# Scan of a hybrid layer: full-width products of raw C with the state in seven of eight groups, and low parts of 28 weight slices by adding DMAs

## The chip, the cores and the metric

The kernel runs on one core of a Trainium2 chip. The metric is the device time of one execution in microseconds; three runs of the kernel before gave a median of 1357.88. Beside these there is one profiled execution with a trace, on which all rows below rest. Engines are named as in the profile: PE (TensorE, with PEld for its weight loads), DVE (VectorE), ACT (ScalarE), POOL (GpSimd) and SP, which here issues most DMAs.

## The reference

One inference step of one layer: 512 frames of a new stream ("prompt") and 64 frames of an old one ("sample"), 576 columns together. A combined projection `h @ w_in` feeds a sparse attention branch and a Mamba-2 branch. Each branch goes through its own projection and a gate, the sum through an output projection, and a SwiGLU feed-forward follows. The change lies in the Mamba-2 scan, cut here to one group of heads and one chunk:

```
acs   = cumsum(dt * a)                              # per head, along the chunk
y_diag = (C B^T * exp(acs_i - acs_j) [i >= j]) (dt * x)
y_off  = exp(acs_i) * (C h_prev)                     # h_prev: the state before the chunk
h      = exp(acs_last) * h_prev + B^T (w_state * x)
y      = y_diag + y_off + d_skip * x
```

There are 8 groups of 4 heads; a head has 64 channels and a state of 64 x 128. C and B are shared by the 4 heads of a group. The prompt starts with a state of zero, the sample with one from memory.

## The kernel before, in words

The program is written as a list of operations with their dependences. A planner (`Plan.order`, from line 397) gives each a duration from a cost function, simulates the five queues, and writes the instructions of each engine out in the order that this gives. So every engine's order is fixed before the run, and all instructions carry line 544 of the program in the profile, where they are issued; tiles tell them apart, not lines.

**Weights.** A weight slice of 128x1024 numbers is loaded by SP into one of two raw buffers (`load_raw`, line 588), and split into a high part and a low part of the type that TensorE multiplies fast (`split`, line 595): ACT copies the raw slice to `wh`, and DVE subtracts, `wl = raw - wh`. With `by_dma` the second half goes another way: ACT writes -`wh` into `wl`, and POOL issues a DMA that adds raw to it. There are three `wh` and three `wl`. A projection takes three products, high by high, high by low and low by high. `fetch` (line 628) walks a queue of slices with an index `j`; line 648 sets `by_dma` for 27 <= j < 48. In that queue slices 48 to 79 are, but for one filler, the scan's input weights (four for a group: B, C and two of x), 80 is a late filler, 81 to 88 are the projection of the attention branch, 89 to 104 that of the Mamba-2 branch.

**Scan.** For each group `stage_a` projects and convolves B, C and x, and `stage_b` calls `chunk` (line 1385) for chunks 0, 1, 4, 2, 3; chunks 0 to 3 are the prompt's, of 128 columns, and chunk 4 is the sample's, of 64. `stage_a` of group g + 1 is written between the chunks of group g, so projection matmuls stand between the scan's steps. In `chunk`:

- SP loads `bc`, the cumulated decays of four heads, spread over all 128 partitions (256 KB); POOL masks it into `dec`, and ACT takes four exponentials.
- TensorE multiplies C by B into a bank of `px` (`px<-bcx`), and turns x and B. DVE multiplies `dec` with the product, and makes `xdt` and `xw`.
- If there is a state (`st`, all chunks but 0): ACT takes the exponential of `bc`, and POOL multiplies it with C into `cs`, a copy of C for each of the four heads (line 1415).
- TensorE makes the chunk's state update in columns 256 to 511 of a `py` bank (`ps`, line 1418); POOL decays the old state into a new tile `hst`, and DVE adds `ps` to it (line 1425).
- `products` (line 1428): for each of four heads `xdt` by `dec`, and with a state also `st` by `cs`, into the same 64 rows of the first half of `py`. These use half of the array's columns each (`tile_position`), two heads side by side. The products of two chunks are issued together, as one batch, when everything that they read is there (`ys`, line 1442).
- `outputs` (line 1437): DVE adds `py` to d_skip * x.

After two groups `stage_c` gates and normalises them and stores them in memory. Beside the last group's chunks the attention branch's projection begins.

Of the kernel before, what the change touches and what calls it, by code (L numbers as in the profile page):

```python
# [5 lines left out]
F32 = mybir.dt.float32  # L6
F32R = mybir.dt.float32r
BF = mybir.dt.bfloat16
AF = mybir.ActivationFunctionType
OP = mybir.AluOpType  # L10
# [3 lines left out]
P = 128  # L14
# [8 lines left out]
NG = 8  # L23
# [528 lines left out]
def build(tc, I, O):  # L552
    R = Plan(tc)
    vec, act, pool, pe, sync = R.vec, R.act, R.pool, R.pe, R.sync
# [33 lines left out]
    def load_raw(src, nk, n):  # L588
        raw = wp.tile([P, nk, n], F32, name=f"raw{cnt[0]}", tag="raw", bufs=NRAW)
        sync.dma_start(raw, src)  # L590
        return raw
# [25 lines left out]
    raws, outs, outs_made = {}, {}, []  # L617
# [7 lines left out]
    def misc_spec():  # L625
        specs.append(["misc"])

    def fetch(done, limit=1 << 30):

        while len(outs_made) < len(specs):  # L630
            i = len(outs_made)
            outs_made.append(i)
            queue.extend((i, s) for s in specs[i])
            outs[i] = []
        with R.prio(4000 if done else 0):
            more = True
            while more:
                more = False
                j = state["ld"]
                if j < min(len(queue), limit) and j < state["sp"] + NRAW:  # L640
                    i, s = queue[j]
                    if s == "misc":
                        raw = wp.tile([P, 8, 104], F32, name="rawm", tag="raw", bufs=NRAW)
                        sync.dma_start(raw[:, :, 0:72], kview(w_in[:, C_KI:C_KI + 72]))
                        sync.dma_start(raw[:, :, 72:104], kview(w_in[:, C_DT:C_DT + 32]))
                        raws[j] = (raw, 8, 104)
                    else:
                        raws[j] = (load_raw(*s), s[1], s[2], 27 <= j < 48)
                    state["ld"] += 1
                    more = True  # L650
                j = state["sp"]
                if j < min(state["ld"], limit) and (j < NWH or queue[j - NWH][0] < done):
                    outs[queue[j][0]].append(split(*raws.pop(j)))
                    state["sp"] += 1
                    more = True
# [6 lines left out]


    NE = 2
    misc_spec()
    for a in range(NE):
        fm_spec(w_in, C_G + P * a)
# [177 lines left out]
    for tb in range(5):  # L845
# [5 lines left out]
        for k4 in range(2):  # L851
            p = px(f"pxn{tb}_{k4}")
# [55 lines left out]
    with R.prio(-1500):  # L908
        for tb in range(5):
            n = P if tb < 4 else NS  # L910
            p = pmm(f"pxt{tb}")
# [6 lines left out]
            st = xsp.tile([P, 8, P], F32, name=f"xs{tb}", tag="xs", bufs=5)  # L918
            for k4 in range(2):
                o, i = st[:, 4 * k4:4 * k4 + 4, :n], p[:, k4].rearrange("p (k q) -> p k q", k=4)[:, :, :n]  # L920
# [85 lines left out]
    for i in range(2):  # L1006
        g = gqk[:, i, :]
# [52 lines left out]
    ps = pmm("pmisc")  # L1060
# [3 lines left out]
    ps = ps[:104, :, :TH]  # L1064
    fillers(NE)
    act.activation(mT.rearrange("p (a b) -> p a b", a=2), ps, AF.Copy)
    p = px("pmiscT")
# [3 lines left out]
    p = px("pmiscS")  # L1071
# [92 lines left out]
    p = px("pacs")  # L1164
# [11 lines left out]
    p = [px("pacsTa"), px("pacsTb", "py")]  # L1176
    for c in range(5):
        o, i0 = (p[0][:32, P * c:P * c + P], P) if c < 4 else (p[1][:32, :NS], NS)
# [6 lines left out]
    acs_d = R.dram([32, T], F32, name="acs_d")  # L1185
# [14 lines left out]
    for b in (4, 1, 2, 3):  # L1200
# [4 lines left out]
        s = ix.tile([P, n], F32, name=f"score{b}")  # L1205
        for h in range(NIH // 2 if smp else NIH):
# [3 lines left out]
            for c0, cn in (((0, TH), (TH, TH)) if smp else ((0, n),)):  # L1210
                ps = px(f"pix{b}_{h}_{c0}", "py")
# [148 lines left out]
    sd = R.mkpool("ssd", reuse_waits="tile")  # L1360
# [24 lines left out]
    def chunk(g, c, xbf, bcx, st):  # L1385

        L = P if c < 4 else NS
        i0 = c * P
        nm = f"s{g}_{c}"
        h4 = lambda z: z[:L].rearrange("p (h d) -> p h d", h=4)  # L1390
        bc = sd.tile([P, 4, P], F32, name=nm + "bc", tag="bc", bufs=2)
        sync.dma_start(bc[:, :, :L], acs_d[4 * g:4 * g + 4, i0:i0 + L][None].to_broadcast([P, 4, L]))
        dec = decS if c == 4 else sd.tile([P, 4, P], F32, name=nm + "dec", tag="dec", bufs=2)
        pool.affine_select(dec[:L, :, :L], bc[:L, :, :L], pattern=[[0, 4], [1, L]], compare_op=OP.is_ge, fill=NEG,
                           base=0, channel_multiplier=-1)
        for h in range(4):
            act.activation(dec[:L, h, :L], dec[:L, h, :L], AF.Exp, bias=nacs[:L, c, 4 * g + h:4 * g + h + 1])
        pt = px(nm + "xt")
        pc = pt[:, 384:512]
        xb = xbf[:, :2 * T].rearrange("p (a b) -> p a b", a=2)  # L1400
        bcf = bcx.rearrange("p a b -> p (a b)")
        pe.matmul(pc[:, :L], bcf[:, i0:i0 + P], bcx[:, 1, i0:i0 + L], start=True, stop=True)
        parts = [vec.tensor_tensor(dec[:L, :, :L], dec[:L, :, :L], pc[:L, None, :L].to_broadcast([L, 4, L]), OP.mult)]
        for i in range(3):
            pe.transpose(pt[:, P * i:P * i + P], xbf[:, i * T + i0:i * T + i0 + P] if i < 2 else bcf[:, i0:i0 + P], ident)
        xdt = xdtS if c == 4 else sd.tile([P, 256], F32, name=nm + "xdt", tag="xdt", bufs=2)
        xw = xwS if c == 4 else sd.tile([P, 256], F32, name=nm + "xw", tag="xw", bufs=2)
        bt = btS if c == 4 else sd.tile([P, P], F32, name=nm + "bt", tag="bt", bufs=2)
        for o, s in ((xdt, dtp), (xw, wst)):
            parts.append(vec.tensor_tensor(h4(o), h4(pt[:, 0:256]), s[:L, c, 4 * g:4 * g + 4, None].to_broadcast([L, 4, HD]), OP.mult))  # L1410
        act.activation(bt[:L], pt[:L, 256:384], AF.Copy)
        if st is not None:
            cs = sd.tile([P, 4, P], F32, name=nm + "cs", tag="cs", bufs=2)
            act.activation(bc[:, :, :L], bc[:, :, :L], AF.Exp)
            parts.append(pool.tensor_tensor(cs[:, :, :L], bc[:, :, :L], bcx[:, None, 1, i0:i0 + L].to_broadcast([P, 4, L]), OP.mult))
        py = px(nm + "y", "py")
        ps = py[:, 256:512]
        pe.matmul(ps, bt, xw, start=True, stop=True)
        new = sd.tile([P, 256], F32, name=nm + "h", tag="hst", bufs=6)
        if st is None:  # L1420
            act.activation(new, ps, AF.Copy)
        else:
            pool.tensor_tensor(new.rearrange("p (h d) -> p h d", h=4), st.rearrange("p (h d) -> p h d", h=4),
                               edec[:, c, 4 * g:4 * g + 4, None].to_broadcast([P, 4, HD]), OP.mult)
            vec.tensor_tensor(new, new, ps, OP.add)
        parts += [o for _, o in new.base.writes]

        def products():
            for h in range(4):
                o = py[64 * (h % 2):64 * (h % 2) + 64, P * (h // 2):P * (h // 2) + L]  # L1430
                pe.matmul(o, xdt[:, 64 * h:64 * h + 64], dec[:, h, :L], start=True, stop=st is None,
                          tile_position=(0, 64 * (h % 2)))
                if st is not None:
                    pe.matmul(o, st[:, 64 * h:64 * h + 64], cs[:, h, :L], start=False, stop=True,
                              tile_position=(0, 64 * (h % 2)))

        def outputs():
            for i in range(2):
                vec.scalar_tensor_tensor(xb[:, i, i0:i0 + L], xb[:, i, i0:i0 + L], dcol[:, 2 * g + i:2 * g + i + 1],
                                         py[:, P * i:P * i + L], op0=OP.mult, op1=OP.add)  # L1440

        ys.append((parts, products, outputs))
        if len(ys) == 2 or g == NG - 1 and c > 0:
            both = sum((y[0] for y in ys), [])
            with R.after(both):
                for y in ys:
                    y[1]()
            for y in ys:
                y[2]()
            ys.clear()  # L1450
        return new
# [110 lines left out]
    for g in range(NG):  # L1562
        if g == NG - 1:
            fillers(LATE, sd, 1)
            R.close(sda, hp)
            gtp = R.mkpool("gate", side="right", reuse_waits="tile")
        for i in range(4):
            if i == 2 and g % 2 and g > 6:
                stage_c(g - 1)
            stage_b(g, i)  # L1570
            if i == 1:
                stage_b(g, 4)
            if i == 2 and g > 0 and g % 2 == 0:
                stage_c(*((g - 2, g - 1) if g <= 6 else (g - 1,)))
            if g + 1 < NG:
                stage_a(g + 1, i)
            if 2 <= g < 6 and i > 1:
                with R.prio(-600):
                    k = 2 * (g - 2) + i - 2
                    load_split(sd, o_d[:, k, :], oh[k], ol[k], 2)  # L1580
    stage_c(NG - 1)
    for s, dst in ((0, O["conv_prompt"]), (1, O["conv_sample"])):
# [2 lines left out]
        o = sd.tile([96, P], F32, name=f"cvoT{s}")  # L1585
        act.activation(o, p[:96, :P], AF.Copy)
        sync.dma_start(dst[0, 0].rearrange("j (a b) -> (j a) b", b=P), o)
    R.close(sd)


    t2 = lambda z: z.rearrange("p (a b) -> p a b", a=2)
# [666 lines left out]
```

## Time and profile before

| | |
|---|---|
| median of three runs | 1357.88 us (1356.46 to 1357.9) |
| profiled execution: its own time | 1357.67 us |
| profiled execution: span of the core | 1355.7 us |
| ACT busy | 754.1 us, 56% of the span |
| POOL busy | 245.4 us, 18% of the span |
| DMA queues | 200.31 MB, mean 148 GB/s |

The span is from the first to the last instruction of the core; the time of the execution is measured around it and is 2.0 us longer. The scan stands at about 455 to 780 us of the span, the two branch projections at about 740 to 910. In the profile's groups of instructions the columns are busy time and mean duration of one, then the engine's idle time just before them and who ended it; f32 matmuls leave two records for each product.

### The profile page before, as it was taken

What the parts mean: (1) busy time and instruction counts of PE and PEld (TensorE: products, weight loads), DVE (VectorE), ACT (ScalarE), POOL (GpSimd) and SP (SyncE); (2) the same over time, 40 slices, a digit from 0 to 9 for tenths busy, and PEclk for the clock granted to TensorE, in tenths of its full rate; (3) what the DMA queues carried; (4) which work ended last, traced back from release to release, by engine and by line L of the source; (5) the groups of instructions that cost most, each with busy time, mean ns of one, the idle gap of its engine ahead of it and who ended that gap; (6) DMA issues with size and microseconds to landing.
All of it is one profiled execution on the core that took longest, in us unless ns stands there. A gap on an engine that the chain in (4) does not pass through costs nothing.

```text
span 1355.7 us, 27900 instructions
## 1 busy us (share of the span) xinstructions
PE 1341.3 (99%) x10677; PEld 1306.5 (96%) x10677; DVE 1141.8 (84%) x2307; ACT 754.1 (56%) x1593; POOL 245.4 (18%) x377
## 2 busy tenths in 40 slices
PE   7999999999999999999999999999999999999998
PEld 6999999999999999999999999999999999999998
DVE  5788999887778798888887688867799999878897
ACT  5445333777777666666565342225476666665453
POOL 2312011230310235545463300001000000000000
PEclk9999999999999999999999999999999999999999
DMA  9762435574755464454445698747423343325352
GB/s 302 226 181 83 111 107 156 124 186 106 173 136 123 131 180 115 113 150 128 131 124 172 209 294 253 232 141 246 127 87 101 96 131 102 94 74 141 98 164 63
DMA packets 267877, 200.31 MB, mean 148 GB/s; under 512 B 25488, under 2 KB 239616, under 8 KB 267744
## 3 DMA queue, kind: packets, MB, share of 16 engines
q1 hardware_dynamic: 263056, 183.40, 46.3%
q0 software_dynamic: 4400, 15.00, 5.4%
q8 instruction: 83, 1.36, 0.4%
q14 instruction: 50, 0.41, 0.1%
q10 hardware_dynamic: 288, 0.13, 0.0%
HBM read 157.75 MB, written 28.96 MB: 138 GB/s over the span
## 4 chain that ended last, share of the span: by engine, by line
PE 91%; DVE 5%; DMA 1%; issue 1%; ACT 1%; POOL 1%; SPq 0%; DVEq 0%; POOLq 0%; ACTq 0%
PE mm L544 63%; PE py L544 16%; PE px L544 12%; DVE score L544 1%; DVE m L544 1%; DMA raw<-in_w_in 1%; DVE wl L544 1%; DMA bc<-acs_d 0%; DMA B<-in_w_down 0%; SPq L544 0%; DVE tok L544 0%; DVE xs L544 0%; ACT wh L544 0%; DVE rr L544 0%; ACT wl L544 0%
## 5 line engine op out<-in xcount | busy, mean ns | idle before, releaser
L544 ACT ACTIVATE wh<-raw 128x1024 fp32r<-128x1024 f32 (+3 forms) x144 | 140.6, 979 | 172.5 <-PE mm L544 131.6
L544 PE MATMUL mm<-hTl,wh 128*128 128x288 f32 (+1 forms) x1024 | 232.6, 302 | 1.1 <-DVE hTl L544 1.1
L544 PE MATMUL mm<-hTh,wh 128*128 128x288 f32 (+1 forms) x1024 | 231.2, 303 | 0.6 <-ACT wh L544 0.5
L544 PE MATMUL mm<-hTh,wl 128*128 128x288 f32 (+1 forms) x1024 | 230.0, 302 | 0.0
L544 PEld LDWEIGHTS mm<-hTl,wh 128*128 128x128 f32 (+1 forms) x1024 | 166.7, 188 | 4.1 <-DVE hTl L544 1.8
L544 PEld LDWEIGHTS mm<-hTh,wh 128*128 128x128 f32 (+1 forms) x1024 | 165.7, 188 | 3.8 <-ACT wh L544 0.7
L544 PEld LDWEIGHTS mm<-hTh,wl 128*128 128x128 f32 (+1 forms) x1024 | 165.4, 188 | 1.6 <-issue 0.9
L544 DVE TENSOR_TENSOR wl<-raw,wh 128x1024 fp32r<-128x1024 f32 (+2 forms) x99 | 122.1, 1235 | 27.1 <-ACT wh L544 26.0
L544 POOL DMA_DIRECT2D wl<-raw x23 | 20.9, 907 | 471.2 <-PE px L544 312.9
L544 DVE SCALAR_TENSOR_TENSOR cu<-xc,wc,cu 128x579 f32<-128x579 f32 x96 | 83.3, 868 | 2.0 <-ACT cu L544 1.0
L544 PE MATMUL mm<-wh,hTl 128*128 128x256 f32 x256 | 73.2, 286 | 0.0
L544 PE MATMUL mm<-wl,hTh 128*128 128x256 f32 x256 | 72.5, 284 | 0.0
L544 PE MATMUL mm<-wh,hTh 128*128 128x256 f32 x256 | 72.4, 285 | 0.0
L544 DVE SCALAR_TENSOR_TENSOR aacc<-adr,sil,aacc 128x512 f32<-128x512 f32 x84 | 59.0, 751 | 5.0 <-DMA adr<-in_w_ada 4.9
L544 PE MATMUL mm<-yh,wl 128*128 128x288 f32 x256 | 55.2, 296 | 0.0
L544 PE MATMUL mm<-yh,wh 128*128 128x288 f32 x256 | 55.0, 296 | 0.0
L544 PE MATMUL mm<-yl,wh 128*128 128x288 f32 x256 | 54.9, 296 | 0.0
L544 PE MATMUL mm<-xhS,wh 128*128 128x290 f32 (+1 forms) x248 | 54.8, 296 | 0.0
L544 ACT ACTIVATE P<-lg,mn 128x128 f32<-128x128 f32 (+4 forms) x72 | 41.7, 580 | 22.6 <-DVE mn L544 21.3
L544 ACT ACTIVATE dec<-dec,nacs 128x128 f32<-128x128 f32 x128 | 42.4, 393 | 15.9 <-POOL dec L544 15.9
L544 PE MATMUL mm<-xhS,wl 128*128 128x290 f32 (+1 forms) x232 | 51.2, 296 | 0.0
L544 PEld LDWEIGHTS mm<-wh,hTl 128*128 128x128 f32 x256 | 48.3, 189 | 0.4
(565 smaller groups left out, 4071.7 us busy)
## 6 DMA issues: line engine op xcount, KB each, us to landing
raw<-in_w_in SPq DMA_DIRECT2D x80, 512.0 KB, 4.2
adr<-in_w_ada SPq DMA_DIRECT2D x36, 512.0 KB, 5.4
raw<-in_w_gate_up SPq DMA_DIRECT2D x22, 512.0 KB, 3.8
wl<-raw POOLq DMA_DIRECT2D x21, 512.0 KB, 4.7
rawu<-in_w_gate_up SPq DMA_DIRECT2D x20, 512.0 KB, 3.9
bc<-acs_d SPq DMA_DIRECT2D x32, 256.0 KB, 3.7
raw<-in_w_branch_ssm SPq DMA_DIRECT2D x16, 512.0 KB, 4.7
gate_d<-sg SPq DMA_DIRECT2D x16, 288.0 KB, 2.2
```

Of the source, the lines that this page charges most:

```text
L544: getattr(engines[x.eng], x.fn)(*[real(a) for a in x.args], **{k: real(v) for k, v in x.kw.items()})
```

## The change

It does two things. In groups 0 to 6, for chunks with a state, the copy `cs` is no longer made. TensorE multiplies the state (two blocks of 128 columns, each two heads) by raw C with all of the array, into the half of the `py` bank that held the state update. The decay is applied to the result: `eb` holds the same cumulated decays in the layout of the output, loaded by two DMAs of 64 rows; ACT takes its exponential, DVE multiplies it with the product, and adds that to the output. In group 7 all stays as it was; `cs` now has a pool of its own, opened for that group, where before it lay in the scan's pool.

The second: slices 60 to 87 of the weight queue are split with `by_dma`, beside 27 to 47 as before.

```diff
-                        raws[j] = (load_raw(*s), s[1], s[2], 27 <= j < 48)
+                        raws[j] = (load_raw(*s), s[1], s[2], j in LOWS)
...
+    LOWS = (*range(27, 48), *range(60, 88))
...
-        if st is not None:
-            cs = sd.tile([P, 4, P], F32, name=nm + "cs", tag="cs", bufs=2)
+        whole = st is not None and g < NG - 1
+        if whole:
+            eb = sd.tile([P, 2, P], F32, name=nm + "eb", tag="eb", bufs=2)
+            for r in range(2):
+                sync.dma_start(eb[64 * r:64 * r + 64, :, :L],
+                               acs_d[4 * g + r:4 * g + 4:2, i0:i0 + L][None].to_broadcast([64, 2, L]))
+            act.activation(eb[:, :, :L], eb[:, :, :L], AF.Exp)
+        elif st is not None:
+            cs = csp.tile([P, 4, P], F32, name=nm + "cs", tag="cs", bufs=2)
             act.activation(bc[:, :, :L], bc[:, :, :L], AF.Exp)
             parts.append(pool.tensor_tensor(cs[:, :, :L], bc[:, :, :L], bcx[:, None, 1, i0:i0 + L].to_broadcast([P, 4, L]), OP.mult))
...
         parts += [o for _, o in new.base.writes]
+        if whole:
+            for i in range(2):
+                pe.matmul(ps[:, P * i:P * i + L], st[:, P * i:P * i + P], bcx[:, 1, i0:i0 + L], start=True, stop=True)
...
-                pe.matmul(o, xdt[:, 64 * h:64 * h + 64], dec[:, h, :L], start=True, stop=st is None,
+                pe.matmul(o, xdt[:, 64 * h:64 * h + 64], dec[:, h, :L], start=True, stop=st is None or whole,
                           tile_position=(0, 64 * (h % 2)))
-                if st is not None:
+                if st is not None and not whole:
                     pe.matmul(o, st[:, 64 * h:64 * h + 64], cs[:, h, :L], start=False, stop=True,
                               tile_position=(0, 64 * (h % 2)))
...
                                          py[:, P * i:P * i + L], op0=OP.mult, op1=OP.add)
+            if whole:
+                vec.tensor_tensor(eb[:, :, :L], eb[:, :, :L], ps.rearrange("p (a l) -> p a l", a=2)[:, :, :L], OP.mult)
+                vec.tensor_tensor(xb[:, :, i0:i0 + L], xb[:, :, i0:i0 + L], eb[:, :, :L], OP.add)
...
             gtp = R.mkpool("gate", side="right", reuse_waits="tile")
+            csp = R.mkpool("cs", side="right", reuse_waits="tile")
...
-    R.close(sd)
+    R.close(csp, sd)
```

## The prediction, made before the changed kernel was run

> **What bounds the kernel now.** I read the page first (busy shares, granted clock), then the windows, cut to the length of one scan group, because a share of the whole span is a mean over stages.
>
> ```profile
> span 1355.7 us, 27900 instructions
> ...
> PE 1341.3 (99%) x10677; PEld 1306.5 (96%) x10677; DVE 1141.8 (84%) x2307; ACT 754.1 (56%) x1593; POOL 245.4 (18%) x377
> ...
> PEclk9999999999999999999999999999999999999999
> ```
>
> ```profile
> core 0: us, PE busy (x) PEld busy (x) DVE busy (x) ACT busy (x) POOL busy (x), PEclk, DMA share, GB/s
> 470.00:520.00 50.00, 50.00 (x407) 48.92 (x405) 44.27 (x76) 32.76 (x74) 15.32 (x32) 1.00 0.57 155
> 557.00:594.00 37.00, 36.68 (x319) 35.11 (x318) 31.08 (x62) 20.97 (x53) 16.91 (x31) 1.00 0.44 128
> 706.00:740.00 34.00, 34.00 (x302) 32.91 (x302) 29.16 (x58) 19.81 (x49) 14.44 (x24) 1.00 0.49 143
> 740.00:780.00 40.00, 39.46 (x349) 36.72 (x348) 24.73 (x53) 14.46 (x30) 12.87 (x14) 1.00 0.72 229
> 780.00:830.00 50.00, 50.00 (x389) 49.62 (x389) 43.50 (x70) 18.84 (x27) 1.17 (x1) 1.00 0.90 289
> ```
>
> TensorE is busy for all of the scan, and its clock is full throughout. Of the rows above only two have a gap: 0.32 us in 557 to 594 and 0.54 us in 740 to 780. DVE stands at 84 to 89%, ACT near 60%, POOL below half, and none of them makes TensorE wait. But busy isn't the same as well used, so the second question is whether TensorE's time there is work at its own pace. The chain of waits answers it: it shows what each run of matmuls takes until the next one starts.
>
> ```profile
> 452.46 21.60 PE mm L544 x162
> ...
> 488.41 1.51 PE py L544 x24
> ...
> 619.01 0.22 PE px L544 x2
> ...
> 621.11 1.95 PE py L544 x32
> ...
> 631.85 0.17 PE px L544 x2
> ...
> 645.73 1.54 PE py L544 x32
> ...
> 768.53 1.07 PE py L544 x16
> ```
>
> A projection matmul takes 21.60/162 = 0.133 us, and this pace holds throughout. The scan's own products come in batches ("py"); a product has two records. 16, 24 and 32 records take 1.07, 1.51 and 1.95 us: 0.44 us for every 4 products more, so **0.11 us a product and 0.19 us fixed per batch**. So the time is the sum of TensorE's instructions in order. A change here is worth what it adds to or takes from that sum, plus at most the 0.86 us of gaps just named; work moved between DVE, POOL, ACT and the DMA queues counts only if TensorE is made to wait.
>
> **The products.** In groups 0 to 6, 28 chunks have a state to multiply (7 groups, chunks 1, 2, 3 and the sample chunk 4): 21 of 128 columns, 7 of 64. Each loses four half-width products of `cs` and gains two full-width ones of raw C.
>
> ```profile
> L544 PE MATMUL py<-cs,hst 128*64 128x128 f32 x192 | 20.5, 273 | 0.0
> ...
> L544 PE MATMUL py<-cs,hst 128*64 128x64 f32 x64 | 4.6, 222 | 0.0
> ```
>
> ```profile
> 618.85 0.38 PE L544 MATMUL px<-bcx 128*128 128x128 f32 x2
> ...
> 631.68 0.33 PE L544 MATMUL px<-bcx 128*128 128x64 f32 x2
> ```
>
> The groups are for all eight groups, two records a product (24 and 8 chunks with a state); their durations overlap, so I price by steps of the chain. The trace has a full-width f32 product with the very operand C on the moving side: `px<-bcx`, at 618.85 with 128 columns and at 631.68 with 64. The chain gives them 0.22 (at 619.01) and 0.17 (at 631.85).
> - 128 columns: removed 4 x 0.11 = 0.44, added 2 x 0.22 = 0.44. **Nothing**, 21 times: two half-width tiles side by side already filled the array.
> - 64 columns: a batch of 32 records with a sample chunk in it takes 1.54 instead of 1.95, so its eight narrow products take 0.41/8 = 0.05 less, 0.06 each. Removed 4 x 0.06 = 0.24, added 2 x 0.17 = 0.34: **+0.10 us, 7 times, +0.7 us**.
> - The batches stay: they still hold the `dec` products, 18 of them touch groups 0 to 6, each with its fixed 0.19.
>
> The price of two full products in a row is bounded below by half of 0.22 a piece (as if one pass did: -0.22 x 21 = -4.6 us in all) and above by the step of 0.43 that the 256-column `py<-xw` takes (x2: +0.42 x 28 = +11.8 us). I take 0.22 and 0.17, the rows with the same shape and the same operand. [...]
>
> **The new wait on TensorE.** The full products write the half bank that DVE has just read for the new state, so they wait for `hst`. The batch had to wait for the same instruction, and TensorE's list of waits has none on `hst` in the whole span. Behind a late one stand all projection matmuls; the order of work puts others between. I take nothing; if all 28 were late by one DVE instruction of 0.41 us, it would be 11.6 us.
>
> **DVE, ACT, POOL.**
>
> ```profile
> L544 DVE TENSOR_TENSOR wl<-raw,wh 128x1024 fp32r<-128x1024 f32 x34 | 42.3, 1245 | 9.0 <-ACT wh L544 8.7
> ...
> L544 DVE SCALAR_TENSOR_TENSOR xb<-xb,dcol,py 128x128 f32<-128x128 f32 x61 | 18.0, 339 | 8.2 <-PE py L544 8.0
> ...
> L544 DVE TENSOR_TENSOR hst<-hst,py 128x256 f32<-128x256 f32 x31 | 12.8, 414 | 5.6 <-PE py L544 5.1
> ```
>
> ```profile
> L544 ACT ACTIVATE wl<-wh 128x1024 fp32r<-128x1024 f32 x21 | 22.0, 1051 | 0.1
> ```
>
> ```profile
> L544 POOL TENSOR_TENSOR cs<-bc,bcx 128x512 f32<-128x512 f32 (+1 forms) x32 | 43.3, 1353 | 11.4 <-ACT bc L544 8.4 <-PE py L544 1.7 <-POOL hst L544 0.9
> ```
>
> ```profile
> L544 POOL DMA_DIRECT2D wl<-raw x23 | 20.9, 907 | 471.2 <-PE px L544 312.9
> ```
>
> DVE gains two instructions a chunk: about 0.41 each at 256 elements (like `hst`), 0.34 at 128: 3 x 0.82 + 0.68 = 3.1 us a group. It loses 28 low parts of 1.245 us: 4 a group is 5.0. Net -1.9 us a group once the low parts are moved. The first group gets the new work only: 44.27 + 3.1 of 50, 95%. Still covered. ACT gains 28 x 1.05 for the negated copies and loses about half of each chunk's second exponential: some +3.5 us a group on 21 of 37. POOL loses 28 `cs` at 1.35 and gains 28 issues at 0.91. All hidden behind TensorE; uncovered, DVE's 3.1 us in the first group would be the largest.
>
> **The DMA queues.** Slices 60 to 87 are the weights of groups 3 to 7, one late filler, and seven of the eight slices of the attention branch. SP issues them, two of them in one row, here:
>
> ```profile
> 511.73 6.17 SPq L544 DMA_DIRECT2D raw<-in_w_in  x2
> ...
> 705.79 0.42 SPq L544 DMA_DIRECT2D raw<-in_w_branch_attn  x1
> ...
> 771.15 0.39 SPq L544 DMA_DIRECT2D raw<-in_w_branch_attn  x1
> ```
>
> Counting 20 slices back from the last one of `in_w` gives slice 60 at 511.73, so the low parts move from then on; the branch's eight go out from 705.79 to 771.15, one every 9.3 us.
>
> ```profile
> q0 software_dynamic: 4400, 15.00, 5.4%
> ...
> wl<-raw POOLq DMA_DIRECT2D x21, 512.0 KB, 4.7
> ...
> bc<-acs_d SPq DMA_DIRECT2D x32, 256.0 KB, 3.7
> ...
> raw<-in_w_branch_attn SPq DMA_DIRECT2D x8, 512.0 KB, 5.1
> ```
>
> ```profile
> SPq L544 <- DMA wl<-raw: 86.3, 17, 16.9
> ...
> SPq L544 <- POOL cs L544: 61.5, 23, 7.7
> ```
>
> The queue of the adding DMAs takes 5.4% of the span for 15 MB, 73 us; a slice of 0.52 MB is 2.6 us of all 16 engines. Four of them a group bring the share of 0.44 to 0.49 to about 0.75, with the new `eb` loads (half of `bc`) to about 0.8; in 740 to 780 it goes from 0.72 to 0.98. At 0.90 (780 to 830) TensorE ran without a gap. A raw buffer, of which there are two, is now held from its load until the sum has landed: 5.1 + 1.05 + 1.05 + 0.91 + 4.7 = 12.8 us (a negated copy and the first copy cost ACT the same), and two serve a slice every 6.4 us, while TensorE takes 9.3. Hidden. On SP the load waits for `wl<-raw` to land, as it did 17 times in the attention stage, and behind it stand the next `bc`, `eb`, `zt` and state loads; against that, `bc` no longer waits for POOL's `cs` (61.5 us of SP's waits). `eb` waits for DVE's last addition of two chunks before, `bc` and weights behind it. POOL's issue waits for ACT's copy, and behind it stand the masking of `dec` and the state's decay.
>
> **The sum**, against the profiled execution's own 1357.67 (1355.7 span and 2.0 around it): +0.7 for the sample chunks, 0 elsewhere, 1358.4. That execution is 0.2 below the median of 1357.88, so **1358.6**.
>
> **The rivals.**
> 1. *Late slices, slower.* Place: 706 to 780, where the adding DMAs meet the loads of the branch at a share near 1. Point: the chain of 12.8 us must grow past two periods of 9.3, 18.6 us; so load and sum, 9.8 together, would have to take over 15.6. Price: beyond it TensorE waits for each of seven slices, about 1 us each at a sum of 17.6: +7, 1365. For it: the share of 0.98, and that the chain leaves TensorE for a load there already (4.97 us of `bc`, at the gap of 0.54):
>
> ```profile
> 748.93 4.97 DMA bc<-acs_d
> ```
>
> Against: three slices ready ahead.
> 2. *The batches lose their fixed part, faster.* If 0.19 comes from a `cs` product that follows `dec` on the same half of the array, and not from entering and leaving half-width mode, 18 batches save it: 18 x 0.19 = 3.4 us, 1355.2 with the sample chunks' 0.7. For it: every batch fitted had such pairs, so the line can't tell the two apart. Against: the timeline of one batch of 16.
>
> ```profile
> 752.50 0.30 PE L544 MATMUL mm<-oh,wh 128*128 128x288 f32 x1
> 752.73 0.45 PE L544 MATMUL py<-dec,xdt 128*64 128x128 f32 x4
> ...
> 753.44 0.44 PE L544 MATMUL py<-cs,hst 128*64 128x128 f32 x4
> 753.81 0.44 PE L544 MATMUL px<-ident,xb 128*128 128x128 f32 x2
> ```
>
> It starts 0.23 after the projection matmul before it, whose step is 0.133, and what follows starts 0.37 after the last four records, whose step is 0.22: 0.10 on entering and 0.15 on leaving, as much as the fixed part. [...]
> 3. *The change doesn't do what it says: full products at half the price*, the lower bound above: 1357.9 + 0.7 - 4.6 = 1354.0. Against: `px<-bcx` has two records a product, as a full f32 product would.
>
> **How the numbers follow.** About 0.2% (2.7 us) is what a measurement of this kernel can tell from no change: 1355.2 to 1360.6. The forecast gets 0.56 (1356.5 to 1360.5), rival 1 with late `hst` and DVE's first group 0.24, rival 2 0.14, rival 3 with a luckier order 0.06. So faster 0.20, same 0.56, slower 0.24. The range, 1354.5 to 1363, leaves out rival 3 and the dearer half of rival 1.
>
> **What would show it.** Right: `py` batches shrink to 16 records at 1.07 with 0.22 and 0.17 for each full product; TensorE without new gaps from 470 to 780; DVE down by some 13 us (28 x 1.245 less 7 x 3.1), POOL by about as much. Rival 1: TensorE waiting for `wl` or `wh` after 706, and `wl<-raw` landing late. Rival 2: batches of 16 records at 0.88. Wrong altogether if TensorE gets gaps on `hst` or `eb`, or if its busy time falls by several us.

## The result, and the profile after

The changed kernel takes **1371.87 us** (median of 6 runs, 1368.85 to 1382.99), the kernel before 1357.41 in the same comparison: a ratio of 1.0124, 95% interval 1.0086 to 1.0162. It is slower by some 14.5 us. The forecast was 1358.6, with a range up to 1363. The profiled execution took 1373.08 us.

The page of the changed kernel: span, busy shares, shares of the chain of waits, the queue of the adding DMAs, and their issues with the median time to landing.

```profile
span 1371.3 us, 27883 instructions
...
PE 1346.4 (98%) x10565; PEld 1310.1 (96%) x10565; DVE 1127.4 (82%) x2335; ACT 774.8 (57%) x1621; POOL 226.7 (17%) x377
...
q0 software_dynamic: 8432, 29.68, 11.0%
...
PE 77%; DVE 11%; DMA 5%; ACT 3%; issue 2%; POOL 1%; SPq 1%; DVEq 0%; ACTq 0%; POOLq 0%
...
wl<-raw POOLq DMA_DIRECT2D x49, 512.0 KB, 5.3
```

DVE has lost 14 us (13 were forecast) and POOL 19 ("about as much" was forecast), and neither shortens the run: TensorE's share of the chain of waits fell to 77% from the 91% of the page of before:

```profile
PE 91%; DVE 5%; DMA 1%; issue 1%; ACT 1%; POOL 1%; SPq 0%; DVEq 0%; POOLq 0%; ACTq 0%
```

The windows say where. Before:

```profile
515.00:700.00 185.00, 184.60 (x1599) 176.85 (x1597) 161.01 (x304) 116.97 (x287) 96.18 (x158) 1.00 0.47 129
...
740.00:800.00 60.00, 59.46 (x501) 56.71 (x500) 41.06 (x81) 24.27 (x45) 14.04 (x15) 1.00 0.76 239
```

After:

```profile
515.00:700.00 185.00, 175.28 (x1414) 167.29 (x1413) 138.03 (x297) 122.64 (x286) 74.28 (x147) 0.98 0.72 176
...
740.00:800.00 60.00, 58.36 (x486) 55.32 (x485) 35.47 (x81) 30.67 (x62) 20.99 (x25) 1.00 0.94 254
```

TensorE (first busy column) stands still for 9.7 us between 515 and 700 us, where the adding DMAs work beside the scan, and for 1.6 in 740 to 800. The share of the DMA engines in the first of these windows rose from 0.47 to 0.72. A useful milestone is the start of the last product of high input by low weight of the scan (tile `wl`, operand `hTh`): 737.9 us before, **752.0 after**. From there to the first product of `mh` by a low weight it is 173.5 us before and 175.1 after. So nearly all was lost inside the scan, not in the branch projections. The milestone is read from one profiled execution of each run, and the order moves it by up to 3 us (e16 and e18 below reach it 1.7 and 2.7 us earlier than before, and are no faster). By the pages the span grew by 15.6 us: TensorE's idle time by 10.5, its busy time by 5.1. Of the 5.1, 1.7 is the slow clock shown below and 0.2 to 0.9 the products (e16 and e18); the rest was not itemised.

One gap shows how. The chain of waits of the changed kernel, 646 to 657 us (start, duration, who), then ACT's and PE's rows of the timeline behind it, the time in brackets being idle before the row:

```profile
646.44 0.53 SPq L544
...
647.03 8.04 DMA eb<-acs_d
...
655.44 0.07 ACT eb L544
...
655.76 0.67 ACT cth L544
656.43 0.28 ACT sto L544
656.75 1.49 PE px L544 x20
```

```profile
655.44 0.42 ACT L544 ACTIVATE eb<-eb 128x256 f32<-128x256 f32 x1 [6.37 <-DMA eb<-acs_d]
```

```profile
656.75 0.68 PE L544 MATMUL px<-ssum,pick 128*32 128x128 f32 x8 [5.59 <-ACT sto L544]
```

SP issues the two loads of `eb`, 64 KB each, from 646.4 us on; the second lands 8 us later. Just before, SP had stood for 7.0 us until an adding DMA landed, and from 644.4 on it issued a weight slice, two loads of `bc` and these two, all within 3.2 us. ACT's next instruction in its fixed order is the exponential of `eb`, which needs them. Nothing else of ACT may pass: `cth` and `sto`, for which everything is there, stand behind it, and TensorE needs `sto`. So TensorE stands for 5.59 us before work that has nothing to do with `eb`. The lists of waits give the sums for 515 to 785 us, first SP's, then ACT's, then TensorE's (total, times, longest); in e1 below, which has no new adds, SP never waits for one:

```profile
SPq L544 <- DMA wl<-raw: 57.6, 17, 7.6
```

```profile
ACT eb L544 <- DMA eb<-acs_d: 22.6, 9, 6.4
```

```profile
PE px L544 <- ACT sto L544: 8.2, 3, 5.6
...
PE py L544 <- DVE hst L544: 0.8, 1, 0.8
```

And the gap costs more than its length. In windows of 2 us the last columns are granted clock, DMA share and GB/s:

```profile
652.00:654.00 2.00, 0.00 (x0) 0.00 (x0) 0.00 (x0) 0.00 (x0) 0.00 (x0) 0.85 0.41 92
654.00:656.00 2.00, 0.00 (x0) 0.00 (x0) 0.00 (x0) 0.56 (x2) 0.00 (x0) 0.50 0.02 5
656.00:658.00 2.00, 1.25 (x20) 1.21 (x20) 1.20 (x4) 0.98 (x3) 0.00 (x0) 0.50 0.19 52
658.00:660.00 2.00, 2.00 (x9) 1.54 (x7) 0.71 (x3) 0.94 (x1) 0.00 (x0) 0.50 0.87 204
660.00:662.00 2.00, 2.00 (x23) 1.88 (x23) 0.56 (x3) 1.49 (x5) 1.27 (x2) 0.94 0.26 77
```

The mean of 0.85 in the first row is 0.6 us at half clock, so the clock fell at about 653.4, 2.3 us into the gap. After the gap TensorE works for some 3.4 us (656.75 to about 660.2) at half its clock, which is another 1.7 us.

### The profile page after: what moved, and what is told of

It is laid out like the page before. It is cut to its first block, busy times and chain, and to the rows that moved or that the text cites. A ratio compares the mean times of both kernels' runs of the same rounds, so it can differ in the third digit from the quotient of the medians.

```text
span 1371.3 us, 27883 instructions
## 1 busy us (share of the span) xinstructions
PE 1346.4 (98%) x10565; PEld 1310.1 (96%) x10565; DVE 1127.4 (82%) x2335; ACT 774.8 (57%) x1621; POOL 226.7 (17%) x377
## 4 chain that ended last, share of the span: by engine, by line
PE 77%; DVE 11%; DMA 5%; ACT 3%; issue 2%; POOL 1%; SPq 1%; DVEq 0%; ACTq 0%; POOLq 0%
PE mm L544 51%; PE py L544 16%; PE px L544 11%; DVE score L544 3%; DVE m L544 2%; DMA eb<-acs_d 2%; DVE cu L544 1%; DMA stage<-y_d 1%; DVE wl L544 1%; DVE xb L544 1%; SPq L544 1%; DMA raw<-in_w_branch_attn 1%; DMA wl<-raw 1%; ACT wh L544 1%; DMA adr<-in_w_ada 0%
## 5 line engine op out<-in xcount | busy, mean ns | idle before, releaser
L544 PE MATMUL mm<-hTh,wl 128*128 128x288 f32 (+1 forms) x1024 | 233.7, 303 | 0.0
L544 POOL DMA_DIRECT2D wl<-raw x51 | 45.5, 893 | 498.7 <-PE px L544 314.5
L544 DVE TENSOR_TENSOR wl<-raw,wh 128x1024 fp32r<-128x1024 f32 (+2 forms) x71 | 87.1, 1230 | 12.3 <-ACT wh L544 10.5
L544 ACT ACTIVATE wl<-wh 128x1024 fp32r<-128x1024 f32 (+1 forms) x51 | 53.4, 1050 | 0.1
```

Of the source, the lines that this page charges most:

```text
L544: getattr(engines[x.eng], x.fn)(*[real(a) for a in x.args], **{k: real(v) for k, v in x.kw.items()})
```

## The experiments

All times are medians against the kernel before on the same chip (1356.1 to 1356.5 us); "scan end" is the milestone above, 737.9 before and 752.0 after.

| run | what runs | us | ratio, 95% interval | scan end |
|---|---|---|---|---|
| e1 | products only | 1359.04 | 1.0023 (1.0013 to 1.0032) | 738.3 |
| e2 | adds only, 28 slices | 1368.49 | 1.0094 (1.008 to 1.0107) | 746.6 |
| e5 | adds only, 7 branch slices | 1358.62 | 1.0014 (1.0005 to 1.0023) | 737.7 |
| e6 | adds only, 21 scan slices | 1366.63 | 1.0072 (1.0059 to 1.0084) | 748.1 |
| e3 | whole change, `eb` from `bc` | 1365.37 | 1.0071 (1.0059 to 1.0084) | 743.4 |
| e4 | products only, `eb` from `bc` | 1361.36 | 1.0039 (1.0027 to 1.0052) | 739.9 |
| e7 | ACT's copies, DVE adds, no DMA | 1364.77 | 1.0058 (1.0046 to 1.0071) | 737.7 |
| e8 | e3 with a third raw buffer | 1366.97 | 1.0074 (1.006 to 1.0088) | 743.0 |
| e10 | whole change, four `eb` | 1375.12 | 1.0134 (1.012 to 1.0147) | 749.3 |
| e11 | before, with idle traffic of 512 KB a slice | 1365.37 | 1.0067 (1.0053 to 1.008) | 746.0 |
| e12 | before, with idle traffic of 64 KB a slice | 1363.63 | 1.0046 (1.0034 to 1.0059) | 740.8 |
| e13 | before, order with room | 1357.32 | 1.0003 (0.9994 to 1.0012) | 738.5 |
| e16 | products only, order with room | 1357.7 | 1.0012 (1.0003 to 1.0021) | 736.2 |
| e18 | products only, order with less room | 1357.77 | 1.0014 (1.0005 to 1.0023) | 735.2 |
| e17 | adds only, 21 scan slices, order with room | 1358.98 | 1.0019 (1.001 to 1.0028) | 739.8 |
| e9 | whole change, order with room | 1367.5 | 1.008 (1.0067 to 1.0093) | 739.9 |
| e14 | whole change, order with more room | 1367.06 | 1.0077 (1.0065 to 1.009) | 742.0 |
| e15 | e3, order with room | 1364.42 | 1.006 (1.0048 to 1.0073) | 742.8 |

### Which half of the change costs

e1 is the changed kernel with the low parts as before; e2, e5 and e6 are the kernel before with adding DMAs for all 28 slices, for the branch's or for the scan's.

```diff
-    LOWS = (*range(27, 48), *range(60, 88))
+    LOWS = range(27, 48)                                            e1
-            raws[j] = (load_raw(*s), s[1], s[2], 27 <= j < 48)
+            raws[j] = (load_raw(*s), s[1], s[2], 27 <= j < 48 or 60 <= j < 88)     e2
+            raws[j] = (load_raw(*s), s[1], s[2], 27 <= j < 48 or 81 <= j < 88)     e5
+            raws[j] = (load_raw(*s), s[1], s[2], 27 <= j < 48 or 60 <= j < 81)     e6
```

> The products as in the change, low parts as before (slices 27 to 47 only). Theory A (the eb loads by themselves land late, and ACT's queue stands behind them): most of the loss stays, 1366 to 1372. Theory B (the adding DMAs and the raw buffers they hold): 1358.1, the +0.7 of the sample chunks. Theory C (eb lands late only because the adding DMAs crowd the queues): 1358 to 1360, and the longest wait of ACT on eb is under 2 us instead of 6.4.

> The scan as before with cs, and slices 60 to 87 by adding DMAs. Theory A: 1357.4, no change. Theory B: 1366 to 1372, with TensorE's gaps where the slices are late. Theory C: 1357 to 1360, since no short load stands at the head of ACT's queue but bc, which lands later by a few us.

> Kernel before, with adding DMAs for the seven branch slices 81 to 87 alone. Rival 1 as predicted (the branch's loads between 706 and 780 are late): most of the low parts' 12 us, 1363 to 1368. Theory D (the loss is made in the scan, where the engines' fixed orders stand behind late transfers): 1356 to 1358.

> Kernel before, with adding DMAs for the 20 scan slices 60 to 79 and the late filler 80. Rival 1 as predicted: 1356 to 1358. Theory D: 1364 to 1368, with TensorE's gaps between 540 and 720.

The halves add up (1.0023 by 1.0094 is 1.0117, the whole 1.0124), and the adds carry most. The branch slices, where rival 1 of the prediction had its place, cost 0.14%, and the scan end stays at 737.7; the 21 scan slices cost 0.72% and put it off by 10.2 us. In the changed kernel too, TensorE's waits after 706 us name neither `wl` nor `wh`, which were rival 1's sign. In e6 there is no `eb`, and yet TensorE waits, here for DVE's product `dec` (waits of 515 to 785, and the DMA issues of that window with their median time to landing):

```profile
PE px L544 <- DVE dec L544: 5.9, 8, 1.9
...
wl<-raw POOLq DMA_DIRECT2D x21, 512.0 KB, 5.0
raw<-in_w_in SPq DMA_DIRECT2D x20, 512.0 KB, 4.6
bc<-acs_d SPq DMA_DIRECT2D x26, 256.0 KB, 3.9
```

Late loads are not shown to be what costs here: in the kernel before the slices land after 4.1 us and `bc` after 3.5, and DVE's list of waits in e6 names no load. The two longest gaps, 1.86 us before 603.92 and 1.68 before 683.12, stand behind something else. DVE works without a pause up to the `dec` that ends them, beginning with an instruction that took 3.06 and 3.05 us in place of 0.69 while POOL worked (shown in the last section).

### The loads of eb

e3 and e4 make `eb` from `bc`, which is there anyway, by two exponentials of 64 rows, and load nothing; e4 has no new adds. e10 leaves the loads and gives `eb` four buffers, so that SP can issue them earlier.

```diff
-                sync.dma_start(eb[64 * r:64 * r + 64, :, :L],
-                               acs_d[4 * g + r:4 * g + 4:2, i0:i0 + L][None].to_broadcast([64, 2, L]))
-            act.activation(eb[:, :, :L], eb[:, :, :L], AF.Exp)
+                act.activation(eb[64 * r:64 * r + 64, :, :L], bc[64 * r:64 * r + 64, r:4:2, :L], AF.Exp)
...
-            eb = sd.tile([P, 2, P], F32, name=nm + "eb", tag="eb", bufs=2)
+            eb = sd.tile([P, 2, P], F32, name=nm + "eb", tag="eb", bufs=4)             e10
```

> The whole change, but eb is no longer loaded: ACT takes the two exponentials of 64 rows straight out of bc, which is there for the masking anyway. Theory A: 1358 to 1359, all the loss goes. Theory B: 1368 to 1372, it stays. Theory C: 1358 to 1361, the gaps behind eb go and what bc then waits for remains.

> The products alone, low parts as before, eb out of bc without a load. All three theories: 1358.1 (before plus 0.7 for the sample chunks); with DVE at about 95% of the scan a stall of DVE could add up to 3.1 us a group for those that it can't hide. If this is slower than 1360, the products themselves cost more than their rows, or DVE has become the bound.

> The change with four eb buffers instead of two, so that an eb load needn't wait until DVE has added the one before the last. If eb is late because its load is issued late: 1363 to 1367, like eb out of bc. If it is late because it lands late among the adding DMAs: 1369 to 1373.

Without adds the loads are the better way (1.0023 against 1.0039); beside them they cost 0.5% (1.0124 by 1.0071). So neither `eb` nor the adds explain that part alone: beside the adds the loads land late, and ACT stands in line for them. e3 lies between what its three readings had expected, and e4 above the 1360 us that it was to stay under; why e4 does was not followed up. The DMA issues of 515 to 785 us, first of e1, then of the changed kernel:

```profile
eb<-acs_d SPq DMA_DIRECT2D x34, 64.0 KB, 3.0
```

```profile
eb<-acs_d SPq DMA_DIRECT2D x34, 64.0 KB, 4.8
```

In e1 ACT waits for `eb` 2.6 us in all, in the changed kernel 22.6. With four buffers in e10 ACT still waits 15.8 us for `eb`, and TensorE still has a gap of 5.15 us there. So buffers of `eb` aren't what holds the loads up.

### What of an adding DMA costs

e7 takes the DMA away and leaves ACT's second copy: DVE adds raw to it, as long as the subtraction before. e8 gives e3 a third raw buffer for 18 slices. In e11 and e12 the kernel before keeps its low parts on DVE, and POOL issues for each of the 28 slices a copy from memory to memory that nothing reads or waits for, of 512 KB or of 64 KB.

```diff
+            if by_dma == 2:                                                             e7
+                vec.tensor_tensor(lo, raw, lo.bitcast(F32), OP.add)
...
+        if by_dma == 2:                                                                 e11
+            made = vec.tensor_tensor(lo, raw, hi.bitcast(F32), OP.subtract)
+            with R.after([made]):
+                pool.dma_start(other[128 * (i - 60):128 * (i - 59)], w_ada[0:128, 0:1024])
...
+                pool.dma_start(other[16 * (i - 60):16 * (i - 59)], w_ada[0:16, 0:1024])  e12
...
+        raw = (sd if third else wp).tile([P, nk, n], F32, name=f"raw{cnt[0]}",           e8
+                tag="raw3" if third else "raw", bufs=1 if third else NRAW)
```

> Kernel before; for slices 60 to 87 ACT writes the negated copy as in the change, but DVE adds raw to it: ACT's 28 extra instructions without any more DMAs, POOL issues or longer held raw buffers (DVE's work as before). If ACT's longer order is the cause: 1362 to 1368. If the transfers are (traffic, raw buffers held, issues on POOL): 1356 to 1359.

> The change with eb out of bc (1365.4 in the run above), and a third raw buffer for slices 62 to 79. If loads go out late because the raw buffer is held until the sum has landed: 1358 to 1361. If transfers are slow because more of them run at once, or the loss is in ACT or POOL: 1363 to 1367.

> Kernel before, low parts of 60 to 87 by DVE as there; for each of these slices POOL also issues a DMA of 512 KB from memory to memory that nothing waits for. If the adding DMAs cost by their traffic and their issue on POOL: 1363 to 1368, as the scan's slices alone (1366.6). If by what waits for them (raw buffers, weights late): 1356 to 1359.

> As the traffic run, with 64 KB instead of 512 KB a DMA: the issue on POOL with an eighth of the traffic. If POOL's issue (0.9 us each, and the order behind it) is the cost: like the traffic run. If the traffic is: 1356 to 1359.

The third buffer is worth nothing, but it doesn't take away the wait that it was meant for: in e8 SP stands for the adds as long as in the changed kernel, and e3 differs little (58.6 us).

```profile
SPq L544 <- DMA wl<-raw: 57.6, 16, 7.5
```

So e8 doesn't tell whether the 12.8 us for which a raw buffer is held cost anything.

e7 loses nothing in the scan and 7 us behind it, mainly in two gaps of 1.04 and 3.76 us that are new. The longer is this, and behind it the clock stands at half too (0.50 in 770 to 772 us). Below it stand the load that its chain of waits leads back to, and ACT's row:

```profile
769.67 0.69 PE L544 MATMUL px<-ident,rowsZ 128*128 128x128 f32 x2 [3.76 <-ACT sto L544]
```

```profile
758.66 6.41 DMA bc<-acs_d
```

```profile
765.86 1.28 ACT L544 ACTIVATE dec<-dec,nacs 128x128 f32<-128x128 f32 x4 [4.94 <-POOL dec L544]
```

It is the pattern of `eb` with another load: `bc` lands after 6.41 us, POOL masks it into `dec`, ACT stands for the mask, and `sto`, for which TensorE waits, is behind. No new adding DMA is needed for it.

e11 and e12 are the surprise: transfers that no instruction waits for cost 9 and 7 us. In e11 the weight slices landed after a median of 5.6 us instead of 4.1. But its two largest gaps, 2.17 us before 617.86 and 2.04 before 722.69, come behind stretched DVE instructions as in e6; with the half clock behind each (mean of 0.91 in 615 to 635 us and in 715 to 735, so 1.8 us each) they make most of the 9. The first is this, in place of 0.82, and the new issue on POOL (610.78, 0.54 us) stands in the unbroken run of POOL's work beside it:

```profile
611.24 3.35 DVE L544 SCALAR_TENSOR_TENSOR cu<-xc,wc,cu 128x579 f32<-128x579 f32 x1
```

In e12 the slices landed after 3.9, so late slices don't explain it. Its largest gap is of e7's kind, with this load and this product:

```profile
756.27 6.20 DMA bc<-acs_d
```

```profile
767.06 0.44 PE L544 MATMUL px<-ident,rowsZ 128*128 128x128 f32 x2 [1.82 <-ACT sto L544]
```

With the half clock behind it (0.50 in 768 to 770 us) that is about half of e12's 7 us. The rest, gaps of under 1 us spread over the scan from 575 to 695 us, stays without an explanation. What e7, e11 and e12 have in common is that each has other instructions than before, and so another order on all engines. They weren't tried with the room of the next section.

### An order with room

That left two readings: any newly written order might lose some, or the orders have no room for loads that land later than the planner thinks. The planner gives a load 0.93 us and its bytes at a rate by their form; for `eb` alone on the queue that is 1.2 us, and in e1 it lands after 3.0. These runs tell it that loads into SBUF and adding DMAs land 2.0 us later while the scan is written (3.0 in e14, 1.0 in e18). No work is changed by it, only the order.

```diff
             op.rate = 300e3 if row >= 4096 else 345e3 if row >= 1024 else 250e3 if row >= 512 else 225e3
-            return 0.06, 0.93
+            return 0.06, 0.93 + (self.late if o is not None and o.base.kind == "sbuf" else 0.0)
...
         if fn == "dma_start":
             op.bytes = 4 * n * o.shape[0]
-            return 0.9, 0.93
+            return 0.9, 0.93 + self.late
...
     ykeep = []
+    R.late = 2.0
...
     stage_c(NG - 1)
+    R.late = 0.0
```

> The change, its planner told that in the scan every load into a buffer and every adding DMA lands 2.0 us later than it assumes (the program's work is the same, only the order in which each engine's instructions are written). Theory E (the transfers are late against a fixed order, and engines stand in it): 1358 to 1364, most of the 14 us gone. If the transfers are too many whatever the order: 1368 to 1373.

> The kernel before, nothing of its work changed; only the planner that writes the order is told that loads issued during the scan land 2.0 us later, so another order comes out. Theory A (the order has no room for loads that land late; an order that has the room costs nothing by itself): 1355 to 1359 us, the last hTh,wl product within 2 us of the 737.9 of before. Theory B (any newly written order loses some, because the old one was the best of many): 1361 to 1368 us. If B holds, part of the loss of every kernel here belongs to the new order and not to the work.

> Full products alone (low parts on VectorE as before), with the 2.0 us of room. Theory A: 1356.5 to 1359, the 0.7 us of TensorE instructions that the products add and little else; scan end by 739. Theory B: 1359 or more.

> Full products alone with 1.0 us of room: a third order for the same work (1359.0 without room, 1357.7 with 2.0, of which 1.7 is one wait on a late y at 818). Should the wait at 818 not come up, the sum of TensorE's instructions says 0.4 to 0.7 us over before: 1356 to 1358. It beats before only if the sum is wrong: below 1355.5.

> The adding DMAs of the 21 scan slices alone (products as before), with 2.0 us of room for late landings; without the room 1366.6 us, last hTh,wl product at 748.1. If the lag of the landings was all of it, the room takes it away: scan end by 740, total 1357 to 1359. If the adds cost by themselves (POOL's queue and the chain scale, dec, hst behind it, buffers held longer): scan end 741 to 746, total 1360 to 1364, as the changed kernels with room (742.0 and 742.8).

> The changed kernel, planner told that loads and adding DMAs of the scan land 3.0 us later (2.0 us before: last hTh,wl product at 739.9 in place of 752.0, but 4.5 us and a slow clock lost at 826 to 832 behind a late modulation weight). Theory A: the scan again ends by 743, whatever happens behind it; total 1359 to 1367. Theory B (the 2.0 us order was lucky in the scan): the scan ends at 746 to 752.

> Changed kernel with eb made from bc (no eb loads) and the 2.0 us of room. Theory A: last hTh,wl product by 741 (743.4 without the room), total 1358 to 1363. Theory B: scan end and total as without the room, 743 and 1365.

e13 speaks against the first reading, with one order: the kernel before in a new order costs 1.0003, with an interval around 1. In such orders each half alone loses part of its price. The products go from 1.0023 to 1.0012 and 1.0014 (the intervals overlap), and TensorE has no gap in the scan (window of e16):

```profile
515.00:700.00 185.00, 185.00 (x1517) 179.29 (x1516) 165.93 (x334) 114.04 (x283) 68.06 (x135) 1.00 0.52 139
```

The scan slices alone go from 1.0072 to 1.0019, the scan end from 748.1 to 739.8. The lines of e17 to set beside those of e6 above:

```profile
PE px L545 <- DVE dec L545: 0.9, 1, 0.9
...
wl<-raw POOLq DMA_DIRECT2D x21, 512.0 KB, 5.5
raw<-in_w_in SPq DMA_DIRECT2D x20, 512.0 KB, 4.7
bc<-acs_d SPq DMA_DIRECT2D x26, 256.0 KB, 3.8
```

The transfers land as late as in e6, the adds even later, and three quarters of the 10 us are gone. So what cost there wasn't the traffic itself but the order beside it. That the room did it, and not merely another order, isn't shown: SP's waits for the adds fell from 48.8 us to 19.7 in 515 to 785 us, as the room intends, but the two stretched DVE instructions are gone as well (the longest of that tile takes 1.61 us).

For the whole change the room does the same within the scan, and only there. e9 ends it at 739.9 instead of 752.0, with `eb` still landing after 4.3 us, and ACT's list of waits has none for it. The profiled execution, at 1370.62 us the slowest of its five (the fastest took 1364.70), gives most of that back later. Its windows and the chain of waits at that place:

```profile
515.00:700.00 185.00, 183.37 (x1502) 176.19 (x1500) 147.85 (x317) 129.18 (x299) 75.28 (x156) 1.00 0.78 187
...
816.00:830.00 14.00, 11.33 (x94) 10.38 (x92) 11.73 (x16) 1.21 (x2) 0.00 (x0) 1.00 0.85 275
830.00:850.00 20.00, 18.14 (x116) 18.14 (x117) 15.94 (x27) 4.58 (x7) 0.00 (x0) 0.83 0.70 213
```

```profile
808.62 7.92 DMA adr<-in_w_ada
...
819.41 5.11 DMA adr<-in_w_ada
```

The weights of the modulation (`adr`) land late, DVE sums them up late, TensorE loses 4.5 us, and then works for part of 830 to 850 at a lower clock. e14 loses at the same place, e15 less. Why both halves together put these loads into a bad place, and each half alone doesn't, was not settled. e15 also missed its expectation inside the scan: 742.8, hardly better than 743.4 without room. No run beats the kernel before; e16, e17 and e18 come within 0.2% of it.

## Why the prediction was wrong

**Right: the products change TensorE's own time by almost nothing.** +0.7 us was forecast; with an order that leaves no gap in the scan, the products alone measure 1.3 and 1.4 us over before (e16, e18), and their profiled executions hold 1.7 and 0.7 us of new waits on `yh` in a branch projection. The prices, in the timeline of the changed kernel:

```profile
640.48 0.61 PE L544 MATMUL py<-bcx,hst 128*128 128x128 f32 x4
641.02 1.09 PE L544 MATMUL py<-dec,xdt 128*64 128x128 f32 x16
642.04 0.40 PE L544 MATMUL mm<-hTh,wl 128*128 128x288 f32 x1
```

Two full products take the step of 0.54, which is what 2 x 0.22 and the 0.10 on going over to half-width products give. TensorE's busy time over the whole execution, with the clock at full, says the same: 1341.3 us before, and on the pages of e16 and e18

```profile
PE 1341.5 (99%) x10565; PEld 1308.0 (96%) x10565; DVE 1155.5 (85%) x2363; ACT 750.3 (55%) x1593; POOL 212.2 (16%) x349
```

```profile
PE 1342.2 (99%) x10565; PEld 1309.3 (97%) x10565; DVE 1154.4 (85%) x2363; ACT 750.0 (55%) x1593; POOL 214.1 (16%) x349
```

**Right: the batches keep their fixed part.** The 16 records above take 1.02, not the 0.88 of rival 2. Rival 3, full products at half the price, falls by the step of 0.54.

**Right in the main: the new wait on `hst`, and the shifts between engines.** TensorE waits for `hst` once, 0.8 us, in the changed kernel, and once, 1.7 us, in e9. DVE's -14 us came as forecast, POOL's -19 is more than forecast, and neither shortened the run, as argued.

**Wrong: "and two serve a slice every 6.4 us, while TensorE takes 9.3. Hidden."** This step of the DMA queues asked only whether the slices keep up. They did, as far as the runs show: TensorE waited for no slice after 706 us, and e5 shows the place of rival 1 at 0.14%. What it left without a price was named one sentence later: the loads that stand behind on SP, and the instructions that wait for them. `eb` entered the sum as bytes only ("half of `bc`"), so the sum had 0 for the waits behind the adds and the loads. In place of that step the runs showed this. SP stands for the adds, 57.6 us of it, and beside them loads land later (medians of e1 and of the changed kernel: `eb` 3.0 and 4.8 us, `bc` 4.3 and 4.9, weight slices 4.1 and 4.5). ACT takes its instructions in a fixed order and waits for `eb` at the head of its line, 22.6 us of it. TensorE needs what stands behind. e3 shows that the loads of `eb` carry about half of the loss. The other half comes with the adds alone (e6), mostly in waits for DVE's `dec`. e17 shows that the same transfers cost a quarter of that in another order; what exactly holds DVE up in e6 stays open, but for the two stretched instructions. The prediction had a sign of it before it: in `748.93 4.97 DMA bc<-acs_d` TensorE already waited for a small load, and rival 1 read that row as a matter of weight slices. Its own last sign, "Wrong altogether if TensorE gets gaps on `hst` or `eb`", is what came: the gap of 5.59 us.

**Wrong: "At 0.90 (780 to 830) TensorE ran without a gap."** The row is true, but that stage has no small loads whose result passes through ACT and DVE to TensorE within a few us. A share of busy DMA engines that is harmless for large slices ahead of time says nothing of a stage with loads that come just in time. This is argued, not tested by itself; and in e9 even large slices (`adr`) came late in that very stage.

**Not seen: the clock.** "Its clock is full throughout" held for the kernel before, whose longest gap in the scan is 0.54 us. The gap of 5.59 us added 1.7 us behind it; the shorter ones of the changed kernel, up to 1.58 us, added none.

## What to carry to other kernels

When an order is written out by hand or by a planner, price a new load not by its bytes but by what stands behind the instruction that waits for it, on that instruction's engine, if it lands 2 us late. Before blaming traffic, run the same work in an order with room: it costs nothing here (1.0003), and in e17 it told the cost of an order from the cost of the traffic. Then compare with yet another order without room, which was not done here. And look for the place where the room's gain is given back.

## What the runs showed of the hardware

Some gaps of TensorE left it at half its clock for some of the work behind them, others did not. The 5.59 us gap above did, for 3.4 us of the work; so did one of 3.76 us in e7 (granted clock 0.50 in 770 to 772 us, 0.84 and 0.80 in the windows around it), and one of only 1.86 us in e6. In e2 the clock stayed full after 2.42 us. The rows of e6, then of e2:

```profile
603.92 0.44 PE L544 MATMUL px<-ident,xb 128*128 128x128 f32 x2 [1.86 <-DVE dec L544]
...
606.00:608.00 2.00, 2.00 (x9) 1.91 (x8) 0.82 (x1) 1.45 (x2) 0.47 (x1) 0.50 1.05 288
```

```profile
681.57 0.44 PE L544 MATMUL px<-ident,xb 128*128 128x128 f32 x2 [2.42 <-DVE dec L544]
...
682.00:684.00 2.00, 2.00 (x17) 2.00 (x16) 0.91 (x3) 0.99 (x3) 0.53 (x1) 1.00 0.81 158
```

In the changed kernel the clock fell 2.3 us into the gap. In e7, by the means of its windows, it fell some 3.4 us into the gap and was full again at about 772.8, 3.1 us after TensorE went on. So the length of a gap alone didn't decide here: 1.86 us cost the clock in e6, and 2.42 us didn't in e2.

The loads land later beside the adds, and not by their size: `eb`'s 64 KB land 1.8 us later, its 32 KB (the sample's chunk) 0.6, `bc`'s 256 KB 0.6, a weight slice of 512 KB 0.4 (medians, e1 and the changed kernel). No run here shows what delays them.

Single DVE instructions took four times as long as their like while POOL worked without a break. In e6 POOL works from 597.77 to 600.58, and DVE's row of the timeline, whose like takes 0.69 us (median of 16), is

```profile
598.09 3.06 DVE L544 SCALAR_TENSOR_TENSOR bcx<-cth,cu 128x512 f32<-128x512 f32 x1 [1.96 <-ACT cth L544]
```

It ends 0.57 us after POOL does, whose work there is four instructions without a break. In e6 this happens twice (the other at 677.28, 3.05 us), and e11 has the 3.35 us in place of 0.82 shown above; in the kernel before no instruction of `bcx<-cth,cu` takes longer than 1.14 us. That POOL's work is the cause isn't shown. The long instruction delays the `dec` behind it, for which TensorE waits in e6; the two gaps there and the half clock after the first, taken as the 1.7 us of the changed kernel, make 5.2 us of the 10 that e6 loses, but no run takes the stretch away alone.
